# The first up weight of each next large expert is split before the present activation is transposed

## The chip, the cores and the metric

The kernel runs on one core of a Trainium2 chip. The metric is the device time of one execution in microseconds (us); three runs of the kernel before gave 2371.76 to 2372.97 us, with a median of 2372.91 us.

## What is computed

The reference is a block of three parts on 512 tokens of width 1024, in fp32: a mixer (attention over selected keys beside a state space model), a mixture of 32 experts with four experts for each token, and a second block of two further mixers. The change touches the mixture of experts alone. Cut to what matters, `toks` being the tokens of one expert `e`:

```python
def run_block(args):
    toks, e = args
    xb = h_pad[toks]
    gu = xb @ w_gu[e] + b_gu[e]
    g, u = gu[:, :D_EXPERT], gu[:, D_EXPERT:]
    g = jnp.minimum(g, SWIGLU_LIMIT)
    u = jnp.clip(u, -SWIGLU_LIMIT, SWIGLU_LIMIT)
    act = (u + 1.0) * (g * jax.nn.sigmoid(SWIGLU_ALPHA * g))
    return act @ w_dn[e] + b_dn[e]
```

Each expert's output is multiplied by the tokens' gates and added to their rows. `w_gu[e]` is 1024 x 2048 (8 MB), `w_dn[e]` is 1024 x 1024 (4 MB).

## The kernel before

The experts are ranked by their number of tokens and worked one after the other, each in a *turn*. The 17 ranks 0 to 16 are *large* (up to 128 tokens), the other 15 *small* (up to 64). `TURNS` sets the order: rank 0, then small and large in turn, with two places where two large ones follow each other. So 16 of the turns after the first belong to large experts.

An expert's weights come as 1 MB pieces: eight of `w_gu` (128 rows by 2048 columns each) for the products *up*, four of `w_dn` for the products *down*. `wraw` (L1704) issues a piece's load on SP's queue (L1709) into a ring of 11 buffers, named raw and XU in the profile; a buffer is free again once the piece has been used. The number of the expert is loaded into a register of SP at the start of its turn (`weights(i)`, L1795).

A large expert's products are made of three matmuls with fp32r operands (`mm3`, L387 to L389): the stationary operand, the activation, is held as a high part and a low part `hl`, and the moving operand, the weight, is split in the same way into H and L. `split` (L355) does that for a piece in two halves of 1024 columns: ScalarE casts the half to H (L368), VectorE subtracts H from the raw data to L (L370). H and L have three buffers each; every fourth half goes to a fourth pair, H2 and L2. The four groups of columns of a piece of `w_gu` go to four banks, two from each half; for each bank the order is H, L, H. A small expert's weights are used as they are, with no split (`up64` L1590, `down64` L1619).

A turn `i` (L1843 to L1878) does in this order: the up products of this expert (`up` or `up64`); the split of up to two down pieces of the previous expert, `down.begin`; the first part of the gate function (`glu`); the transposes of the next expert's gathered tokens (`transposed`, L1493, or `turned64`); the down products of the *previous* expert (`down.products`), in the midst of which the gate function is finished (`then`, L1603 and L1604); the selection matrix for the next expert's bias (`selected`, VectorE, L1690 or L1697); the transposes of this expert's activation (`acted` for a large one: eight transposes L1635, evictions on ScalarE L393 and VectorE L394; `turned` for a small one: four transposes L1506, one copy on ScalarE L1507), which the down products of the *next* turn use. `settle` runs `down.end`: the previous expert's output is scaled on VectorE (L1657) and added to its rows by a scatter that POOL issues (L1664). A large turn calls it behind the split of its first up piece (`then` in `up`).

From the second turn on, `inorder` (L305) ties each instruction of TensorE, VectorE and ScalarE to the one before it on its engine, so that these three engines keep the order in which the program is written. SP's and POOL's instructions are not tied.

Of the kernel before, what the change touches and what calls it, by code (L numbers as in the profile page):

```python
# [19 lines left out]
D = 1024  # L20
S = 512
NT = 4
KD = 8
# [7 lines left out]
NBIG = 17  # L31
# [3 lines left out]
def turns():  # L35
    big, small = list(range(1, NBIG)), list(range(NBIG, NE))
    gaps = max(1, len(small) - 1)

    upto = lambda k: (2 * k * len(big) + gaps) // (2 * gaps)
    more = [upto(k + 1) - upto(k) for k in range(gaps)]  # L40
    out = [0]
    for k, r in enumerate(small):
        out.append(r)
        if k < gaps:
            out, big = out + big[:more[k]], big[more[k]:]
    return out


TURNS = turns()
# [217 lines left out]
class Kern:  # L267
# [1292 lines left out]
        nc.vector.tensor_tensor(self.gate[:, r:r + 1], ms[:, :, 1], ms[:, :, 2], op=OP.add)  # L1560
        return u

    def up(self, hl, sel, pieces, pool=(), then=None):


        nc = self.nc
        bs = [self.bank("mm") for _ in range(4)]
        for k, c0, w, n in pieces:
            w = self.split(w(), n, pool=k in pool)
            if then and k == pieces[0][0]:  # L1570
                then()
            x = (hl[:, 0, k * P:(k + 1) * P], hl[:, 1, k * P:(k + 1) * P])
            for i in range(c0 // 512, (c0 + n) // 512):
                self.mm3(bs[i], x, w(i * 512 - c0, 512), k == 0, False)
                if k == KD - 1:
                    nc.tensor.matmul(bs[i], lhsT=sel[:, i // 2], rhs=self.bgu[:, (i % 2) * 512:(i % 2 + 1) * 512], start=False, stop=True)
            self.tick(1)
        return bs
# [168 lines left out]
    def moe(self):  # L1747
        nc, I, c, p = self.nc, self.I, self.c, self.p
        sel = self.sel0
        oh = self.oh0  # L1750
        with self.tc.issue_after(self.first.ins):
            hl = self.rows(oh)
# [26 lines left out]
        def following(i):  # L1779
            if i == 0:  # L1780
                self.route()
                yield
                self.slot(0, self.counted([oh], self.meta, 0, 1))
                yield from fetch(1)
                yield
            yield from fetch(i + 2)
            if TURNS[i] >= NBIG:
                yield from fetch(i + 3)

        def weights(i):  # L1790

            g, d = I["w_gu"][0], I["w_dn"][0]
            if i:
                r = TURNS[i]
                ev = nc.sync.value_load(self.eidi[:1, r:r + 1], min_val=0, max_val=NE - 1)  # L1795
                g, d = (I[n][bass.ds(ev, 1)].rearrange("o k n -> (o k) n") for n in ("w_gu", "w_dn"))
            return lambda k: g[k * P:(k + 1) * P], lambda kk: d[kk * 256:(kk + 1) * 256].rearrange("(p k) n -> p (k n)", k=2)

        def selected(i):
            r = TURNS[i]  # L1800
            return (self.select64 if r >= NBIG else self.select)(self.eid[:, r:r + 1])
# [38 lines left out]
        def settle():  # L1840
            while due:
                due.pop(0)()
        for i, r in enumerate(TURNS):  # L1843
            small = r >= NBIG
            wg, wd = weights(i)
            self.bg = [following(i)]
            with self.inorder(i > 0, (ET.PE, ET.DVE, ET.Activation), order):
                if small:
                    settle()
                    bs = self.up64(hl, sel, wg)  # L1850
                else:
                    with ExitStack() if i else self.tc.issue_after(self.first.ins):
                        bs = self.up(hl, sel, [(k, 0, lambda k=k: self.wraw(wg(k)), 2 * D) for k in range(KD)], then=settle)
                if i == 0:
                    self.rowload(self.gf, self.mrow[3], nc.gpsimd)
                    for h in range(2):
                        row = self.mrow[3]
                        nc.gpsimd.dma_start(self.gf2[64 * h:64 * h + 64], bass.AP(tensor=row.tensor, offset=row.offset + 512 * h, ap=[[0, 64], [1, 512]]))
                self.drain()
                if down:  # L1860
                    down.begin(0 if down.small else 2 if small else 1)
                glus = [self.glu(*bs)] if small else [self.glu(bs[n], bs[2 + n]) for n in range(2)]
                if i + 1 < NE:
                    hl = (self.turned64 if TURNS[i + 1] >= NBIG else self.transposed)(out.pop(i + 1))
                us = []
                then = lambda: us.extend(g() for g in glus)
                if down:
                    down.products(then)
                    due.append(down.end)
                else:  # L1870
                    then()
                osel = sel
                if i + 1 < NE:
                    sel = selected(i + 1)
                    if TURNS[i + 1] >= NBIG:
                        settle()
                ah = self.turned(us[0]) if small else self.acted(us)
                down = Down(r, ah, osel, wd)  # L1878
# [478 lines left out]
```

## Time and profile before

| | before |
|---|---|
| median of the runs | 2372.91 us |
| the profiled execution's own time | 2369.02 us |
| its span in the profile | 2366.8 us |
| VectorE busy | 1523.1 us (64% of the span) |
| ScalarE busy | 984.9 us (42%) |
| GpSimd busy | 309.1 us (13%) |
| bytes that the DMA engines moved | 576.36 MB |
| loads of expert weights | 256 of `w_gu`, 128 of `w_dn`, 1 MB each |

The profile names the engines PE (TensorE), PEld (its weight loads), DVE (VectorE), ACT (ScalarE), POOL (GpSimd) and SP (SyncE, which issues the loads). All times in it are counted from the start of the span. The expert stage lies between about 650 and 1705 us. A tile name such as H or raw stands for all of its buffers. The granted clock is a share: 1.00 is full speed, 0.50 half.

### The profile page before, as it was taken

What the parts mean: (1) busy time and instruction counts of PE and PEld (TensorE: products, weight loads), DVE (VectorE), ACT (ScalarE), POOL (GpSimd) and SP (SyncE); (2) the same over time, 40 slices, a digit from 0 to 9 for tenths busy, and PEclk for the clock granted to TensorE, in tenths of its full rate; (3) what the DMA queues carried; (4) which work ended last, traced back from release to release, by engine and by line L of the source; (5) the groups of instructions that cost most, each with busy time, mean ns of one, the idle gap of its engine ahead of it and who ended that gap; (6) DMA issues with size and microseconds to landing.
All of it is one profiled execution on the core that took longest, in us unless ns stands there. A gap on an engine that the chain in (4) does not pass through costs nothing. (4 is left out here: it accounts for less than half of the span.)

```text
span 2366.8 us, 28018 instructions
## 1 busy us (share of the span) xinstructions
PE 2224.0 (94%) x10217; PEld 1592.0 (67%) x10217; DVE 1523.1 (64%) x2471; ACT 984.9 (42%) x1371; POOL 309.1 (13%) x177
## 2 busy tenths in 40 slices
PE   5999999999799999999999999999879999999898
PEld 4676667677665566656566666665458888888676
DVE  7678778863866668766667667666451534448864
ACT  4424444332444436444444445444242422336652
POOL 3011102421111100101100010011010111101210
PEclk9999999999899999999999999999979999999999
DMA  7332344652899999999999998999732222222220
GB/s 303 99 106 103 122 158 164 242 176 87 328 390 372 400 402 393 353 387 388 392 405 396 398 403 336 378 407 393 292 145 74 103 83 82 88 83 96 91 87 36
DMA packets 93938, 576.36 MB, mean 244 GB/s; under 512 B 12591, under 2 KB 14361, under 8 KB 32611
## 3 DMA queue, kind: packets, MB, share of 16 engines
q1 hardware_dynamic: 79856, 540.60, 58.4%
q0 software_dynamic: 8432, 18.21, 3.1%
q10 hardware_dynamic: 5508, 15.71, 1.8%
q8 instruction: 82, 1.34, 0.2%
q14 instruction: 60, 0.49, 0.1%
HBM read 556.74 MB, written 27.59 MB: 247 GB/s over the span
## 5 line engine op out<-in xcount | busy, mean ns | idle before, releaser
L370 DVE TENSOR_TENSOR L<-raw,H 128x1024 fp32r<-128x1024 f32 x478 | 590.1, 1259 | 286.1 <-ACT H L368 277.3
L368 ACT CAST H<-raw 128x1024 fp32r<-128x1024 f32 x501 | 515.6, 1049 | 396.2 <-PE mm L389 179.4
L387 PE MATMUL mm<-H,hl 128*128 128x512 f32 x544 | 223.4, 411 | 25.9 <-ACT H L368 25.9
L388 PE MATMUL mm<-L,hl 128*128 128x512 f32 x544 | 225.0, 414 | 14.3 <-DVE L L370 14.3
L389 PE MATMUL mm<-H,hl 128*128 128x512 f32 x544 | 222.2, 408 | 0.0
L387 PE MATMUL mm<-U,H 128*128 128x512 f32 (+1 forms) x488 | 187.6, 384 | 3.0 <-DVE U L708 3.0
L388 PE MATMUL mm<-U,H 128*128 128x512 f32 (+1 forms) x488 | 186.6, 382 | 0.0
L389 PE MATMUL mm<-U,L 128*128 128x512 f32 (+1 forms) x488 | 185.7, 382 | 0.0
L1590 PE MATMUL mm<-raw,sx 128*64 128x512 f32 x792 | 180.3, 598 | 0.0
L387 PE MATMUL mm<-E,H 128*128 128x512 f32 x416 | 173.6, 420 | 3.7 <-ACT E L393 3.7
L387 PE MATMUL mm<-H,U 128*128 128x512 f32 x424 | 170.0, 401 | 2.3 <-DVE w L2256 1.1
L389 PE MATMUL mm<-H,U 128*128 128x512 f32 x424 | 168.2, 397 | 0.4 <-DVE U L394 0.4
L388 PE MATMUL mm<-E,H 128*128 128x512 f32 x416 | 167.0, 402 | 1.5 <-DVE E L394 1.4
L388 PE MATMUL mm<-L,U 128*128 128x512 f32 x424 | 168.3, 397 | 0.0
L389 PE MATMUL mm<-E,L 128*128 128x512 f32 x416 | 166.3, 400 | 0.0
L387 PEld LDWEIGHTS mm<-H,hl 128*128 128x128 f32 x544 | 107.0, 197 | 53.0 <-ACT H L368 29.0
L388 PEld LDWEIGHTS mm<-L,hl 128*128 128x128 f32 x544 | 107.5, 198 | 45.6 <-DVE L L370 21.0
L1599 ACT ACTIVATE w<-w 128x512 f32<-128x512 f32 x49 | 31.0, 632 | 248.4 <-DVE w L1598 248.4
L389 PEld LDWEIGHTS mm<-H,hl 128*128 128x128 f32 x544 | 107.7, 198 | 23.7
L1590 PEld LDWEIGHTS mm<-raw,sx 128*64 128x64 f32 x792 | 54.1, 137 | 98.6 <-issue 94.5
L370 POOL TENSOR_TENSOR L<-raw,H 128x1024 fp32r<-128x1024 f32 x23 | 55.2, 2401 | 444.5 <-ACT H L368 444.5
L388 PE MATMUL at<-L,hl 128*128 128x512 f32 x272 | 108.2, 398 | 2.3 <-DVE L L370 2.3
(443 smaller groups left out, 3843.0 us busy)
## 6 DMA issues: line engine op xcount, KB each, us to landing
raw<-in_w_gu_dram SPq DMA_DIRECT2D x212, 1024.0 KB
raw<-in_w_dn_dram SPq DMA_DIRECT2D x103, 1024.0 KB
XU<-in_w_gu_dram SPq DMA_DIRECT2D x44, 1024.0 KB
XU<-in_w_dn_dram SPq DMA_DIRECT2D x25, 1024.0 KB
raw<-in_win_dram SPq DMA_DIRECT2D x20, 1024.0 KB
raw<-in_w_ada_dram SPq DMA_DIRECT2D x16, 1024.0 KB
raw<-in_wug_dram SPq DMA_DIRECT2D x16, 1024.0 KB
raw<-in_wxg_dram SPq DMA_DIRECT2D x12, 1024.0 KB
```

The source lines that it names most:

```text
L368: nc.scalar.copy(h[:, :m], src)
L370: eng.tensor_tensor(l[:, :m], src, h[:, :m].bitcast(F32), op=OP.subtract)
L387: t.matmul(out, lhsT=lhs[0], rhs=rhs[0], start=start, stop=False)
L388: t.matmul(out, lhsT=lhs[0], rhs=rhs[1], start=False, stop=False)
L389: t.matmul(out, lhsT=lhs[1], rhs=rhs[0], start=False, stop=stop)
L1590: nc.tensor.matmul(bs[i // 2][64 * (i % 2):64 * (i % 2) + 64], lhsT=x[:, k], rhs=w[:, i * 512:(i + 1) * 512], start=False, stop=k == KD - 1)
L1599: nc.scalar.activation(s, g, AF.Sigmoid, scale=1.702)
```

## The change

Behind the down products of a turn, if there is a next turn, the kernel now makes the next expert's `weights`; if that expert is large, it also issues the load and the split of its first `w_gu` piece there, ahead of `selected`, of `settle` and of the transposes of the present activation. `up` gets the split piece as `head` and uses it in place of its own first split. The number of instructions stays the same.

```diff
-    def up(self, hl, sel, pieces, pool=(), then=None):
+    def up(self, hl, sel, pieces, pool=(), then=None, head=None):
...
         for k, c0, w, n in pieces:
-            w = self.split(w(), n, pool=k in pool)
+            w = head if head and k == pieces[0][0] else self.split(w(), n, pool=k in pool)
...
+        head, ahead = None, weights(0)
         for i, r in enumerate(TURNS):
             small = r >= NBIG
-            wg, wd = weights(i)
+            wg, wd = ahead
...
-                        bs = self.up(hl, sel, [(k, 0, lambda k=k: self.wraw(wg(k)), 2 * D) for k in range(KD)], then=settle)
+                        bs = self.up(hl, sel, [(k, 0, lambda k=k: self.wraw(wg(k)), 2 * D) for k in range(KD)], then=settle, head=head)
...
-                osel = sel
+                osel, head = sel, None
                 if i + 1 < NE:
+                    ahead = weights(i + 1)
+                    if TURNS[i + 1] < NBIG:
+                        head = self.split(self.wraw(ahead[0](0)))
                     sel = selected(i + 1)
                     if TURNS[i + 1] >= NBIG:
                         settle()
```

## Rows read from the trace of the kernel before

**Rows 1.** The page: TensorE's busy time, and its granted clock in 40 slices.

```profile
PE 2224.0 (94%) x10217; PEld 1592.0 (67%) x10217; DVE 1523.1 (64%) x2471; ACT 984.9 (42%) x1371; POOL 309.1 (13%) x177
PEclk9999999999899999999999999999979999999999
```

**Rows 2.** Waits of TensorE, 660 to 1700 us: who waited for whom, total, times, longest.

```profile
PE mm L387 <- ACT H L368: 25.9, 16, 1.6
PE mm L388 <- DVE L L370: 14.3, 20, 0.8
PE at L388 <- DVE L L370: 2.3, 2, 1.2
```

**Rows 3.** Time line of TensorE, 880 to 891 us: start, length, what, [idle before].

```profile
883.10 0.40 PE L389 MATMUL at<-H,hl 128*128 128x512 f32 x1
...
886.35 0.63 PE L1506 MATMUL at<-cst,w 128*128 128x128 f32 x4
888.60 0.50 PE L387 MATMUL mm<-H,hl 128*128 128x512 f32 x1 [1.62 <-ACT H L368]
889.86 0.50 PE L388 MATMUL mm<-L,hl 128*128 128x512 f32 x1 [0.76 <-DVE L L370]
```

**Rows 4.** Time line of ScalarE, 878 to 892 us.

```profile
881.10 1.05 ACT L368 CAST H<-raw 128x1024 fp32r<-128x1024 f32 x1 [0.41 <-PE at L389]
887.02 0.58 ACT L1507 COPY sx<-at 128x512 f32<-128x512 f32 x1 [4.87 <-PE at L1506]
887.50 3.89 ACT L368 CAST H<-raw 128x1024 fp32r<-128x1024 f32 x4
```

**Rows 5.** Time line of VectorE, 878 to 893 us.

```profile
882.43 2.35 DVE L370 TENSOR_TENSOR L<-raw,H 128x1024 fp32r<-128x1024 f32 x2
884.70 0.35 DVE L1690 TENSOR_SCALAR sel<-rc,eid 128x256 fp32r<-128x256 f32 x1
888.58 2.36 DVE L370 TENSOR_TENSOR L<-raw,H 128x1024 fp32r<-128x1024 f32 x2 [3.53 <-ACT H L368]
890.86 1.40 DVE L1657 SCALAR_TENSOR_TENSOR w<-at,gate,gf 128x512 f32<-128x512 f32 x2
892.18 1.21 DVE L370 TENSOR_TENSOR L<-raw,H 128x1024 fp32r<-128x1024 f32 x1
```

**Rows 6.** Time line of TensorE, 826 to 828 us, at another large turn's second weight.

```profile
826.07 0.40 PE L387 MATMUL mm<-H,hl 128*128 128x512 f32 x1
826.30 0.39 PE L388 MATMUL mm<-L,hl 128*128 128x512 f32 x1
...
827.69 0.51 PE L388 MATMUL mm<-L,hl 128*128 128x512 f32 x1 [0.53 <-DVE L L370]
```

**Rows 7.** 12 us from a gap: busy us (instructions) by engine, PEclk, DMA share, GB/s.

```profile
885.30:897.30 12.00, 9.62 (x36) 7.45 (x35) 8.72 (x9) 7.75 (x9) 2.32 (x1) 0.86 1.01 420
...
1060.90:1072.90 12.00, 9.62 (x31) 7.36 (x30) 8.29 (x8) 6.82 (x8) 2.33 (x1) 0.72 1.02 423
...
1194.80:1206.80 12.00, 9.08 (x40) 6.85 (x39) 8.65 (x9) 8.41 (x9) 2.33 (x1) 1.00 1.01 423
```

**Rows 8.** Time line of TensorE, 1064 to 1072 us, behind another gap.

```profile
1067.38 0.63 PE L389 MATMUL mm<-H,hl 128*128 128x512 f32 x1
1067.81 0.63 PE L387 MATMUL mm<-H,hl 128*128 128x512 f32 x1
```

**Rows 9.** The expert stage and two stretches of 20 us in it, columns as above.

```profile
660.00:1690.00 1030.00, 987.40 (x4446) 635.46 (x4447) 694.27 (x904) 470.81 (x530) 101.30 (x59) 0.98 0.98 388
...
760.00:780.00 20.00, 20.00 (x86) 16.20 (x86) 17.32 (x16) 12.62 (x12) 2.34 (x1) 0.97 1.02 400
...
1120.00:1140.00 20.00, 17.62 (x70) 13.84 (x69) 15.71 (x19) 12.51 (x15) 2.33 (x1) 0.91 1.01 420
```

**Rows 10.** Waits of SP's queue, 660 to 1690 us.

```profile
SPq L1709 <- DVE L L370: 420.5, 163, 6.2
```

**Rows 11.** Time line of SP, 860 to 876 us.

```profile
862.07 7.89 SPq L1709 DMA_DIRECT2D raw<-in_w_gu_dram  x5
```

**Rows 12.** Waits of ScalarE, 660 to 1700 us.

```profile
ACT H L368 <- DMA raw<-in_w_dn_dram: 27.0, 18, 3.6
```

## The prediction

> **What bounds the kernel now.** I read the page first, then the waits of TensorE, then the time line around one of them, then the transfers. TensorE is busy for 94% of the span, and its clock is granted in full over most of it [rows 1]. The chain that ended last goes back only to 1717.86 us, behind the expert stage, so it says nothing of the change and the stage has to be read by its waits. Between 660 and 1700 us TensorE's matmuls waited 25.9 us in 16 places for a cast of a weight on ScalarE, and 14.3 us in 20 places for a subtract on VectorE; there is little else [rows 2]. Sixteen is the number of turns that lead into a large expert. So TensorE sets the pace of the stage, and it loses it at the start of each large expert.
>
> One such place shows why. TensorE issues the last matmul of the third down weight at 883.10, works through the fourth, turns the activation at 886.35 with four transposes that last until 886.98, and then idles 1.62 us until the first weight's H half is there (888.60) and 0.76 us more for its L half [rows 3]. ScalarE was done with its last cast at 882.15 and stood idle for 4.87 us: the program order puts the copy of the turned activation first, and that copy needs the transposes. Only behind it come the casts of the first weight [rows 4]. VectorE idled 3.53 us for the same reason [rows 5].
>
> **The change, part by part.** Moved per large turn: one 1 MB load (its issue), two casts of 1.05 us and two subtracts (2.36 us together [rows 5]), from behind the transposes' evictions to ahead of them. Nothing is added or removed.
>
> *ScalarE.* Halves of a weight go in turn through three H buffers and one H2, so each is free again two weights later: the head needs what the third down weight held, whose last matmul ends at about 883.5 [rows 3]. ScalarE, idle from 882.15, can cast the head by about 884.9 (883.5, a wake-up of 0.4 as in the gap of [rows 4], 1.05), still 1.4 us before the transposes are issued. The copy behind it on ScalarE stays where it is.
>
> *VectorE.* It ends the fourth down weight's subtracts at 884.78; the head's two follow until 887.14, then the selection (0.35), the previous expert's output (1.40), and the first subtract of the second weight (1.21) until 890.10 [rows 5]. Late by this is only the selection, which the eighth weight's products need, far off; the previous expert's output, and POOL's scatter behind it, come 3.4 us earlier.
>
> *TensorE* finds H and the first L half (about 886.0) ready when the transposes end at 886.98. Both waits go: 16 x 1.62 = **25.9 us**, and the 0.77 us waits. Of the 14.3 us, four waits of 0.53 stand elsewhere (next paragraph), so 14.3 - 2.1 = **12.2 us**.
>
> *What is late next*: the second weight. Its second matmul would be issued at 886.98 + 13 x 0.23 = 890.0, and its L half is ready at 890.10, so some 0.2 us of wait. Today four of the sixteen places, those without the loss of clock below, wait 0.53 us there [rows 6]. I set this term to nothing; its ends are 16 x 0.2 = 3 us lost and 16 x 0.53 = 8.5 us won.
>
> *The clock.* After 12 of the 16 gaps the granted clock fell to half (1.2 instead of 2.4 GHz), and after none of the four others. In the 12 us from each gap, ten places have a mean clock of 0.86, two have 0.72 and four have 1.00. The places at 1.00 issued 39 or 40 matmuls, those at 0.86 about 3 fewer, those at 0.72 about 8 fewer [rows 7]. At 0.23 us each [rows 6] that is 10 x 3 x 0.23 + 2 x 8 x 0.23 = **10.6 us**. TensorE idles before each of these falls, so I take them to go with the gaps. Ends: nothing, if they come anyway; or 10 x 3.4 + 2 x 6.7 = 47 us at half clock (0.14 and 0.28 of 12 us, doubled), in which a matmul takes 0.43 instead of 0.23 us [rows 6, 8]: 47 x 0.46 = 22 us.
>
> *SP and POOL.* The register load of the next expert's number and the first weight's load are moved past no instruction of SP: between their old and new place stand only work of VectorE, ScalarE and TensorE, and the scatter on POOL. I cost this at nothing. The cover is the lead of the loads: the weight cast at 887.50 was issued at 862.07, 25 us before [rows 4, 11]. Without it the cast would wait for data, as the down weights' casts do now, 27.0 us in 18 places [rows 12].
>
> *The transfers.* They move 388 GB/s over the stage at a share of 0.98 [rows 9]. A stage 48.7 us shorter needs 388 x 1030 / 981 = 407 GB/s. Stretches of 20 us with a share above 1 show 400 to 420 [rows 9]. That is close, but SP's waits are for buffers (VectorE 420.5 us) [rows 10] and TensorE never waits for data there [rows 2], and the lead of 25 us can be eaten before it does. I take nothing; the other end is the second rival. The Trainium skill (HBM Reference, Specifications (TRN2)) gives an effective 358 GB/s per core, and about 425 for a core that streams alone; the 388 to 420 here agree with the second. By the first the loads would be at their limit already and the change would give nothing, by the second they stay clear.
>
> **Sum**: 25.9 + 12.2 + 10.6 = 48.7 us off the profiled 2369.0, which is 3.9 us below the median of the runs. Carried to the median: 2372.9 - 48.7 = **2324**.
>
> **Rivals.** (1) *As above*, 2324; own range from all of 25.9 + 14.3 + 22 = 62 us (2311) to a clock that falls anyway, 38.1 us (2335). Chance 0.66.
> (2) *The transfers become the bound.* If 400 GB/s [rows 9] is what they can do with the gathers and scatters among them, the stage loses only 1030 x (1 - 388/400) = 31 us: 2342. For it: the share near 1. Against: the lead, and the higher rows. 0.14.
> (3) *VectorE becomes the bound at the second weight.* If its chain is later than I work out, by the 0.77 of today, the wait for L moves one weight on and TensorE still idles enough for the clock to fall: only 25.9 us go, 2347. For it: just 0.1 us separate the two sums. Against: VectorE starts its subtracts 3.8 us earlier. 0.12.
> (4) *No change.* The transfers already set the pace, and what TensorE doesn't wait for here it waits for data later: 2373. Against it: no wait for data in [rows 2]. 0.04. By the 358 GB/s of HBM Reference (the Trainium skill, Specifications (TRN2)) it would come out so; the 388 GB/s of the stage [rows 9] speak against it.
> (5) *Slower: the head waits for its data.* The cast now stands ahead of the activation's eviction on ScalarE. Should the ring of loads run dry, so that the first weight lands over 2.4 us after the transposes end, each turn costs more than it saves. At the longest wait for data now, 3.6 us [rows 12], that is 16 x (3.6 - 2.4) = 19 us more: 2392. It takes the loss of a 25 us lead. 0.04.
>
> **How the numbers follow.** About 0.2% (4.7 us) is what a measurement of this kernel can tell from no change. Faster: (1), (2) and (3), 0.92; same: (4), 0.04; slower: (5), 0.04. The range runs from 2311, the far end of (1), to 2345, which takes in (2) and most of the way to (3); what lies outside is (4), (5) and part of (3).
>
> **What would show it.** Right: the 16 waits of L387 for the cast gone from TensorE's waits, the L388 waits for the subtract at 16 times 0.2 or less, the casts of the first weight ahead of the copy of the turned activation on ScalarE, no half clock between 690 and 1600 us, some 407 GB/s over the stage. Wrong: waits of a cast for w_gu data (2 or 5), L388 waits of 0.5 us and more at the second weight (3), or half clock without a gap before it.

## The result, and the profile after

| | before | after |
|---|---|---|
| median of the runs | 2371.35 us (6 runs) | 2343.82 us (6 runs, 2341.84 to 2347.54) |
| ratio to before, 95% interval | | 0.9888 [0.9875, 0.9902] |
| the profiled execution's own time | 2369.02 us | 2344.60 us |
| its span in the profile | 2366.8 us | 2342.4 us |
| the stage, share and rate of the transfers | 0.98, 388 GB/s [rows 9] | 1.00, 399 GB/s |

The change gains 27.5 us, where I forecast 48.7. The direction and the range were right, the size was not: 2343.8 is the time of rival (2), in which the transfers become the bound (2342). The page of the changed kernel shows little of this; TensorE's busy time, which answers to [rows 1], fell by 4.9 us, and the row of its clock looks much the same: slices of 59 us are too coarse for what happened.

```profile
PE 2219.1 (95%) x10217; PEld 1586.3 (68%) x10217; DVE 1519.0 (65%) x2471; ACT 983.1 (42%) x1371; POOL 295.3 (13%) x177
PEclk9999999999799999999999999999889999999999
...
q1 hardware_dynamic: 79856, 540.60, 58.7%
q0 software_dynamic: 8432, 18.21, 3.1%
```

The last two lines are the queue of the large loads and that of the gathers and scatters: packets, MB, share of the span on 16 engines. 18.21 MB take 3.1% (73 us of the span), 540.60 MB take 58.7%.

The waits of TensorE, 650 to 1700 us (who waited for whom, total us, times, longest), answer to [rows 2]:

```profile
PE at L388 <- DVE L L370: 13.9, 19, 1.2
PE at L387 <- ACT H L368: 8.9, 8, 1.5
PE mm L388 <- DVE L L370: 1.8, 2, 0.9
```

The 16 waits of an up product for its cast are gone, and so are the 0.76 us waits for the L half behind them. (The two waits left of an up product, 0.91 us each, stand at the second weight of the two large turns that directly follow a large one.) In their place stand 27 waits of the *down* products (`at`), 22.8 us, where [rows 2] have two of 2.3 us. The time line of TensorE around the place of [rows 3], one turn that lies 7 us earlier now, shows both:

```profile
872.86 0.40 PE L389 MATMUL at<-H,hl 128*128 128x512 f32 x1
873.88 0.50 PE L387 MATMUL at<-H,hl 128*128 128x512 f32 x1 [0.62 <-ACT H L368]
875.14 0.50 PE L388 MATMUL at<-L,hl 128*128 128x512 f32 x1 [0.76 <-DVE L L370]
...
881.38 0.63 PE L1506 MATMUL at<-cst,w 128*128 128x128 f32 x4
881.77 0.47 PE L387 MATMUL mm<-H,hl 128*128 128x512 f32 x1
882.08 0.39 PE L388 MATMUL mm<-L,hl 128*128 128x512 f32 x1
```

From the transposes to the first up matmul it is 0.39 us now (881.38 to 881.77), as forecast with no gap, and to the second 0.31. But the third down weight (873.88) comes late. ScalarE's time line says why:

```profile
863.77 1.99 ACT L368 CAST H<-raw 128x1024 fp32r<-128x1024 f32 x2 [13.10 <-DMA raw<-in_w_dn_dram]
867.21 2.00 ACT L368 CAST H<-raw 128x1024 fp32r<-128x1024 f32 x2 [1.45 <-DMA raw<-in_w_dn_dram]
871.29 0.63 ACT L1599 ACTIVATE w<-w 128x512 f32<-128x512 f32 x1 [2.08 <-DVE w L1598]
871.83 1.05 ACT L393 CAST hl<-at 128x512 fp32r<-128x512 f32 x2
872.77 4.88 ACT L368 CAST H<-raw 128x1024 fp32r<-128x1024 f32 x5
...
882.05 0.58 ACT L1507 COPY sx<-at 128x512 f32<-128x512 f32 x1 [3.01 <-PE at L1506]
```

The cast of the first down piece waited 13.10 us for the piece to land. ScalarE works in program order, so the gate function (871.29; it waited 2.08 us for VectorE, which stood behind the subtracts of these pieces), an eviction (871.83) and the casts of the later down pieces (872.77) run late behind it. The copy of the turned activation (882.05) does stand behind the head's casts, as the change asks. Over the stage, such waits of ScalarE have grown from 27.0 us, longest 3.6 [rows 12] (and 8.3 us, longest 2.7, for pieces in XU), to:

```profile
ACT H L368 <- DMA raw<-in_w_dn_dram: 139.5, 22, 15.4
...
ACT H L368 <- DMA XU<-in_w_dn_dram: 37.5, 6, 15.9
```

What SP waited for before it could issue a load, 650 to 1700 us, is the clearest sign. In [rows 10] its largest wait was for VectorE to free a buffer. Now the two largest are for earlier loads to land:

```profile
SPq L1709 <- DMA raw<-in_w_gu_dram: 209.6, 119, 4.3
SPq L1709 <- DMA raw<-in_w_dn_dram: 174.9, 80, 3.7
SPq L1709 <- PE mm L1590: 113.8, 73, 13.4
SPq L1709 <- DVE L L370: 95.7, 75, 5.0
```

With the buffers in XU, SP's waits for earlier loads come to 471.3 us, where the kernel before has 3.1; from 650 to 800 us there are none.

So two things happened: the gaps went, and the loads became the pace of the stage. The experiments separate the two.

### The profile page after: what moved, and what is told of

The parts are those of the page before. It is cut to its first block, busy times and chain, and to the rows that moved or that the text cites. A ratio compares the mean times of both kernels' runs of the same rounds, so it can differ in the third digit from the quotient of the medians.

```text
span 2342.4 us, 28018 instructions
## 1 busy us (share of the span) xinstructions
PE 2219.1 (95%) x10217; PEld 1586.3 (68%) x10217; DVE 1519.0 (65%) x2471; ACT 983.1 (42%) x1371; POOL 295.3 (13%) x177
## 2 busy tenths in 40 slices
DMA packets 93938, 576.36 MB, mean 246 GB/s; under 512 B 12591, under 2 KB 14361, under 8 KB 32611
## 3 DMA queue, kind: packets, MB, share of 16 engines
q1 hardware_dynamic: 79856, 540.60, 58.7%
q0 software_dynamic: 8432, 18.21, 3.1%
## 5 line engine op out<-in xcount | busy, mean ns | idle before, releaser
L388 PE MATMUL mm<-L,hl 128*128 128x512 f32 x544 | 215.3, 396 | 1.8 <-DVE L L370 1.8
L387 PE MATMUL mm<-H,hl 128*128 128x512 f32 x544 | 215.5, 396 | 0.0
L389 PE MATMUL mm<-H,hl 128*128 128x512 f32 x544 | 214.1, 394 | 0.0
L388 PE MATMUL mm<-U,H 128*128 128x512 f32 (+1 forms) x488 | 186.9, 383 | 0.0
L388 PE MATMUL mm<-E,H 128*128 128x512 f32 x416 | 167.6, 403 | 1.5 <-DVE E L394 1.4
L388 PE MATMUL mm<-L,U 128*128 128x512 f32 x424 | 168.7, 398 | 0.0
L388 PE MATMUL at<-L,hl 128*128 128x512 f32 x272 | 112.7, 415 | 14.1 <-DVE L L370 13.9
L388 PEld LDWEIGHTS mm<-L,hl 128*128 128x128 f32 x544 | 102.2, 188 | 29.2 <-DVE L L370 7.1
L387 PE MATMUL at<-H,hl 128*128 128x512 f32 x272 | 111.0, 408 | 8.9 <-ACT H L368 8.9
L387 PEld LDWEIGHTS mm<-H,hl 128*128 128x128 f32 x544 | 102.4, 188 | 22.2
L389 PEld LDWEIGHTS mm<-H,hl 128*128 128x128 f32 x544 | 102.1, 188 | 22.4
```

Of the source, the lines that this page charges most:

```text
L387: t.matmul(out, lhsT=lhs[0], rhs=rhs[0], start=start, stop=False)
L388: t.matmul(out, lhsT=lhs[0], rhs=rhs[1], start=False, stop=False)
L389: t.matmul(out, lhsT=lhs[1], rhs=rhs[0], start=False, stop=stop)
```

## The experiments

My theory (T) was that a gap is worth what I took or more, and that the transfers take back the rest. The rival (R) was that a gap is simply worth less, some 1.7 us instead of 3. All times are medians, and the ratio is taken over all runs, so it can differ a little from that of the two medians. Kernels with the same time in the column "before" were run beside the same runs of the kernel before. That column varies by 2 us, so a difference between kernels of different groups is good to some 2 us.

| kernel | us | before | ratio, 95% interval |
|---|---|---|---|
| few_after | 2302.12 | 2369.36 | 0.971 [0.9694, 0.9726] |
| few_before | 2366.75 | 2369.36 | 0.9988 [0.9978, 0.9999] |
| head_first8 | 2353.30 | 2369.36 | 0.993 [0.9913, 0.9946] |
| head_last8 | 2352.84 | 2369.36 | 0.9927 [0.9911, 0.9944] |
| noscatter | 2304.59 | 2370.14 | 0.9718 [0.9702, 0.9734] |
| spread | 2323.69 | 2370.14 | 0.9805 [0.9788, 0.9821] |
| early3 | 2354.56 | 2370.14 | 0.9934 [0.9917, 0.995] |
| ring4 | 2344.25 | 2370.14 | 0.9891 [0.9874, 0.9907] |
| spread_before | 2369.24 | 2371.38 | 0.9997 [0.9985, 1.0009] |
| spread_alt | 2323.36 | 2371.38 | 0.98 [0.9785, 0.9815] |
| spread_begin1 | 2325.61 | 2371.38 | 0.981 [0.9794, 0.9825] |

### Fewer loads, with the change and without it

On the changed kernel (few_after) and on the kernel before (few_before), 30 of the 384 loads of 1 MB fall away: the second and fourth down piece of each small expert, whose products read the first and third again. The instructions of TensorE, VectorE and ScalarE stay.

```diff
             def piece(d, kk):
-                w = self.wraw(d.wd(kk))
+                if d.small and kk % 2:
+                    return d.kept
+                w = d.kept = self.wraw(d.wd(kk))
                 return w if d.small else self.split(w)
```

> The changed kernel, with the second and the fourth down weight of each small expert left out (its products read the first and third again): 30 of 384 loads of 1 MB fewer, the same matmuls, casts and subtracts. T (the gaps were priced rightly, but the loads of weights became the bound once the lead of the loads was used up): the loads stop binding, so the full price of the gaps appears: 40 to 55 us under the kernel before (2371), with TensorE's waits for casts and subtracts nearly gone and the granted clock full through the stage. R (the gaps and the clock were worth only about half of what I took, and the loads play no part): the same 27 us as the change, within 5.

> The kernel before with the same 30 loads left out (second and fourth down weight of each small expert). T: the kernel before waits for the activation's eviction and not for data, so nothing moves: within 5 us of 2371. Rival D (the loads already held up the kernel before): 15 us or more faster.

Measured: 2302.12 and 2366.75. Without the change the missing loads are worth 0.12% and TensorE's waits stand as in [rows 2]; with it they are worth 41.7 us (2343.82 to 2302.12; 39.7 us with each set against the kernel before of its own group). So the kernel before was not held by its loads, and the changed one is. Between the two kernels with few loads lie 64.6 us: that is what the sixteen gaps cost, more than my 48.7 and more than twice what the change gave. R falls. The stage of few_after keeps no wait for a cast, and its clock never drops behind the start (waits of TensorE, 650 to 1660 us):

```profile
PE at L388 <- DVE L L370: 2.4, 2, 1.2
...
PE mm L388 <- DVE L L370: 1.8, 2, 0.9
```

How the gain goes is seen in three stretches of the stage (columns as in [rows 9]; the number to follow is the count of TensorE's matmuls, the first in brackets). Before:

```profile
640.00:860.00 220.00, 210.28 (x950) 134.62 (x952) 145.75 (x204) 96.87 (x110) 22.88 (x14) 0.98 1.00 391
860.00:1060.00 200.00, 191.68 (x862) 126.20 (x859) 140.72 (x187) 95.46 (x107) 19.05 (x12) 0.97 0.97 379
1060.00:1430.00 370.00, 354.64 (x1597) 226.82 (x1595) 246.02 (x321) 165.39 (x186) 36.19 (x21) 0.98 0.99 396
```

The changed kernel, and its stage as a whole:

```profile
640.00:860.00 220.00, 218.13 (x1010) 138.16 (x1010) 150.90 (x219) 100.01 (x113) 24.05 (x15) 0.99 1.01 401
860.00:1060.00 200.00, 193.96 (x882) 130.77 (x879) 151.61 (x194) 105.99 (x119) 17.94 (x12) 0.99 1.01 404
1060.00:1430.00 370.00, 357.56 (x1615) 227.90 (x1614) 250.57 (x330) 168.48 (x191) 29.94 (x22) 0.98 1.00 398
...
660.00:1665.00 1005.00, 981.49 (x4470) 626.76 (x4470) 693.00 (x907) 469.84 (x532) 90.18 (x60) 0.99 1.00 399
```

few_after:

```profile
640.00:860.00 220.00, 217.81 (x1008) 137.37 (x1006) 148.07 (x213) 101.85 (x116) 24.06 (x15) 0.99 1.00 389
860.00:1060.00 200.00, 197.92 (x910) 136.43 (x910) 159.28 (x200) 108.14 (x120) 20.45 (x12) 1.00 0.98 383
1060.00:1430.00 370.00, 367.92 (x1711) 236.61 (x1711) 263.42 (x349) 179.81 (x204) 38.70 (x23) 1.00 0.98 382
```

In the first 220 us the changed kernel does as much as few_after (1010 and 1008 matmuls, before 950). Then the lead of the loads is used up: 882 to 910 (before 862), and from 1060 to 1430 us 1615 to 1711, hardly more than the 1597 of before. (Some records of matmuls may be missing, and a cut falls in another part of a turn in each kernel, so a difference of some twenty means nothing.) The share of the transfers tells the cases badly apart: 0.98 stands in the stage before, which they did not bind, and in few_after.

### One half of the turns alone

```diff
-                    if TURNS[i + 1] < NBIG:
+                    if TURNS[i + 1] <= 8:
```

for head_first8, and `8 < TURNS[i + 1] < NBIG` for head_last8: each has eight of the 16 heads.

> The change at the first eight of the sixteen large turns alone (ranks 1 to 8). T: the stage gains some 4 us a turn until the lead of the loads is used up after five to six turns, and keeps that: 19 to 25 us under the kernel before. R (each gap is worth 27/16 = 1.7 us): 14 us, within 3.

> The change at the last eight of the sixteen large turns alone (ranks 9 to 16). T: the lead of the loads is still whole when they come, and the pair of large turns among them gives some of it back: 22 to 30 us under the kernel before, about as much as all sixteen. R: 14 us, within 3.

Measured: 16.1 and 16.5 us won, 8 waits of 1.62 us left in each. T's sizes are missed on both; by these two runs alone R would have stood, and it is few_after that rules it out. The halves sum to 32.6, over the 27.5 of both together, which is T's sign, but each gives half and not nearly all. The likely reason is that the limit is local: head_first8 has already fallen to 879 matmuls between 860 and 1060 us (the changed kernel 882), and what its loads have to spare in the second half can't be fetched ahead, because the ring holds 11 pieces. I have not shown that by a run of its own.

### Without the scatters

The output rows of the experts are not added to the tokens; the large loads stay as they are.

```diff
     def scatter(self, o, tok, small=False):
 
+        return
```

> The changed kernel with the 31 scatters that add an expert's output to its rows left out, so that the experts' outputs but the last are missing from the sum. T (the transfers bind): gathers and scatters hold the DMA engines for 3.1% of the span, about 73 us, for 18 MB; without the scatters some 30 us of that go to the weights' loads: 20 to 35 us under the changed kernel (2344), that is 2309 to 2324. Rival B (only the 1 MB loads count, the small packets fit between them): within 5 us of 2344.

Measured: 2304.59, 39 us under the changed kernel and within 2.5 us of few_after. That is more than I expected. TensorE's waits are those of few_after, SP waits for buffers again, and all transfers together run at 402 GB/s over the stage. The third line is the queue that in the changed kernel held the gathers and scatters, with 18.21 MB and 3.1%:

```profile
SPq L1710 <- DVE L L370: 369.5, 159, 5.7
```

```profile
660.00:1640.00 980.00, 975.63 (x4516) 627.68 (x4515) 697.83 (x912) 474.38 (x534) 41.95 (x29) 1.00 0.99 402
```

```profile
q0 software_dynamic: 3968, 9.90, 1.2%
```

So the full set of loads fits into a stage without gaps, if the scatters leave the transfers alone. The scatters are 8.31 of the 18.21 MB of queue q0, 1.4% of all bytes: at the 399 GB/s of the stage they would take 21 us by estimate. But they held the 16 engines for some 45 us (3.1% of 2342.4 us less 1.2% of 2303.1), and without them 39 us come back. Removing them also frees POOL (41.95 us busy, 90.18 with them), but nothing on TensorE waited for it.

### The rows of gathers and scatters spread over the partitions

A token's slot decides the partition in which its row lies. With fewer tokens than slots, the rows fill the first partitions. Here the slots are numbered in bit-reversed order, so that the rows spread over all partitions that a transfer covers (64 in a small expert's gather); rank 0 stays as it was.

```diff
-    parts["iota64"] = np.broadcast_to(i % 64, (P, P))
+    rev = lambda n: np.array([int(format(c, f"0{n}b")[::-1], 2) for c in range(1 << n)])
+    parts["slot64"] = np.broadcast_to(rev(6), (P, 64))
+    parts["slot128"] = np.broadcast_to(rev(7), (P, P))
...
-        return self.nc.vector.tensor_tensor(oh, self.mcc("iota64" if small else "iota128")[:, None, :].to_broadcast([P, NT, P]),
+        if small:
+            return self.nc.vector.tensor_tensor(oh.rearrange("p t (h c) -> p t h c", h=2), self.mcc("slot64")[:, None, None, :].to_broadcast([P, NT, 2, 64]),
+                                                pos[:, :, r:r + 1, None].to_broadcast([P, NT, 2, 64]), op=OP.is_equal)
+        return self.nc.vector.tensor_tensor(oh, self.mcc("slot128" if r else "iota128")[:, None, :].to_broadcast([P, NT, P]),
...
```

> The changed kernel with each expert's tokens put into its slots in bit-reversed order, so that the valid rows of a gather or scatter lie evenly over the partitions instead of in the first ones; the same bytes and instructions. T with uneven engines (the sixteen engines of a transfer serve fixed partitions, and those of the first partitions carry all gathers and scatters, so they finish the loads late): 10 to 30 us under the changed kernel (2344). T with even engines (only the sum of the work on all sixteen counts): within 4 us of 2344. R (transfers play no part): within 4 us.

The same edit on the kernel before is spread_before:

> The kernel before with the bit-reversed slots, without the moved split. T (the loads bind only once the gaps are gone): within 4 us of the kernel before (2370). Rival D (the slots make the kernel faster by themselves, whatever the gaps): some 20 us under it, as the slots gave the changed kernel.

Measured: with the change 2323.69, 20.1 us under the changed kernel; without it 2369.24 against 2371.38, a ratio of 0.9997 [0.9985, 1.0009], no difference. The order of the slots is worth something only where the transfers set the pace, so it acts through them. With spread_alt below, which is as fast, this is the fastest version of the study that computes everything, faster than both kernels. Its stage moves 406 GB/s, 7 more than the 399 of the changed kernel, and SP's waits for earlier loads are fewer, though not gone:

```profile
SPq L1714 <- DMA raw<-in_w_gu_dram: 160.7, 96, 3.2
```

```profile
660.00:1640.00 980.00, 963.59 (x4434) 617.35 (x4434) 685.29 (x898) 464.96 (x526) 93.16 (x60) 1.00 1.01 406
```

Two more runs asked what is left on top of spread. spread_alt has the 64-row gathers of small experts alternate between partitions 0 to 63 and 64 to 127:

```diff
-    def gather(self, gidx):
-
-        x = self.w4()
+    def gather(self, gidx, p0=0):
+
+        x = self.w4()[p0:]
...
-            out[i] = self.gather(self.gidx[:64 if r >= NBIG else P, r:r + 1])
+            p0 = 64 * (r % 2) if r >= NBIG else 0
+            out[i] = self.gather(self.gidx[:64 if r >= NBIG else P, r:r + 1], p0)
...
```

> The changed kernel with bit-reversed slots (2324), in which the gathers of every second small expert also land in partitions 64 to 127 instead of 0 to 63. T with uneven engines: a small gather of some 45 rows then lies on all engines in turn, 4 to 10 us under 2324. T with a gather's rows dealt to the engines by their number: within 3 us of 2324.

spread_begin1 splits only one down piece ahead of the gate function, so that ScalarE's queue stands behind one late load and not two:

```diff
-                    down.begin(0 if down.small else 2 if small else 1)
+                    down.begin(0 if down.small else 1)
```

> The changed kernel with bit-reversed slots (2324), which in a small turn begins one down weight of the previous expert ahead of the gate function instead of two. T (the transfers still set the pace, TensorE's waits in the down products are only where that shows): within 4 us of 2324. Rival Q (the second cast, waiting for its data at the head of ScalarE's queue, holds up the gate function and the evictions behind it, and that costs the 16 us that TensorE waits there): 8 to 16 us under 2324.

Measured: 2323.36 and 2325.61, no gain from either. Which half of the partitions a small gather uses makes no difference here, so of the two forms of T the one with uneven engines misses its 4 to 10 us. spread_begin1 leaves ScalarE's casts waiting for down pieces as long as before (154.6 us, in spread 158.0), because the first piece still stands at the head of its queue; TensorE's waits in the down products stay too (15.7 and 15.8 us). So beginning one piece fewer wins nothing, but whether the blocked queue has a cost of its own beside the late loads is not shown.

### The start of the stage and the depth of the ring

early3 issues the first expert's first three down loads ahead of the routing, to fill the ring earlier:

```diff
-        self.ahead = ahead + [self.wraw(I["w_gu"][0, k * P:(k + 1) * P, :]) for k in range(3, KD)]
+        ahead += [self.wraw(I["w_gu"][0, k * P:(k + 1) * P, :]) for k in range(3, KD)]
+        self.down0 = [self.wraw(I["w_dn"][0, kk * 256:(kk + 1) * 256, :].rearrange("(p k) n -> p (k n)", k=2)) for kk in range(3)]
+        self.ahead = ahead
...
-                w = self.wraw(d.wd(kk))
+                w = self.down0.pop(0) if d.r == 0 and self.down0 else self.wraw(d.wd(kk))
```

> The changed kernel with the first three down weights of the first expert loaded right behind its up weights, ahead of the wait for the routing, in a stretch (620 to 640 us) in which the transfers' share is 0.60, 8 us of idle time. T: the loads are three further ahead, which counts once: 5 to 8 us under the changed kernel (2344). R: within 3 us of it.

Measured: 2354.56, 10.7 us *slower* than the changed kernel: a plain miss. Down pieces of an expert are used a turn after its up pieces, so three of the eleven buffers were held by pieces not yet needed. SP's time line (start, length, what) shows it:

```profile
633.64 18.39 SPq L1709 DMA_DIRECT2D raw<-in_w_gu_dram  x8
673.03 0.34 SPq L1709 DMA_DIRECT2D raw<-in_w_dn_dram  x1
```

Between 652.0 and 673.0 us no load was issued. Once loads set the pace, an idle stretch of theirs is lost for good. From 620 to 700 us the share of the transfers is 0.76, in the changed kernel 0.89, so they idle for some 19 of these 80 us against 9. That difference of 10 us has the size of the loss; no run of its own shows that it is all of it.

ring4 has one buffer fewer, 10 instead of 11:

```diff
-NRAW = 5
+NRAW = 4
```

> The changed kernel with 10 instead of 11 buffers in the ring of loads. T (the rate of the transfers binds, the ring only holds the lead): one transfer less of lead, 2 to 5 us over the changed kernel (2344). Rival L (each transfer's latency binds, so that the loads in flight set the rate): 10/11 of the rate from the point where the loads bind, some 40 us over it or more.

Measured: 2344.25, the same as the changed kernel, so rival L falls, and the 2 to 5 us of T can't be told from nothing. It is the rate of the transfers that binds, not how many are under way. SP's largest wait is for buffers here, though the time is that of the changed kernel:

```profile
SPq L1709 <- DVE L L370: 240.8, 138, 5.7
```

Its waits for earlier loads still come to 237.9 us (before 3.1). So what tells is that such waits are there at all, and not which wait is the largest. A deeper ring, which would lengthen the lead, was not tried on the chip.

## Why the prediction was right in direction and wrong in size

- **TensorE's waits at the first weight** went as worked out, on all 16 turns; ScalarE's and VectorE's order is the one I laid out. Rival (3) came at two turns alone, the 0.91 us waits at the second weight where a large turn follows a large one.
- **The price of a gap** was too small. Three of its terms were short, and the reason is how I read the rows. First, the idle time that a row shows is less than what the wait costs, since a matmul's shown length overlaps the next one (0.40 us long, 0.23 us apart [rows 6]): from the transposes to the first up matmul it took 2.25 us before (886.35 to 888.60) [rows 3] and takes 0.39 now, so 1.86 and not 1.62; to the second 1.26 before and 0.31 now, so 0.95 and not 0.77. Second, I set the second weight's wait to nothing, and the four waits of 0.53 us [rows 6] went too: in few_after only the two waits of L388 on `mm` after a large turn are left. Third, the clock: I counted the matmuls missing in stretches with a fall against the stretches without one, but those are the four that held the second weight's wait, so a part of the loss cancelled out. A half-clock stretch holds some 8 matmuls, each 0.43 instead of 0.23 us apart [rows 6, 8], which is 1.6 us, not 0.7. Worked out again: 10 turns of 1.86 + 0.95 + 1.6, four of 1.86 + 0.95 + 0.53, two with twice the clock's loss, 44.1 + 13.4 + 12.0 = 69.5 us. Measured between the two kernels with few loads: 64.6. This sum was made with the result known; some 2 us of its excess are the two waits left, each 1.1 us from start to start.
- **The clock** falls with the gaps: behind the start of the stage few_before has as many stretches with a fall as the kernel before, few_after none, and the changed kernel five, each behind a new wait of the down products for a cast (1.01 to 1.50 us). Three more of these waits (0.62, 1.04 and 1.20 us) saw no fall, as four of the sixteen gaps before; why is open. The first block shows 12 us from such a place (columns as in [rows 7]), the second TensorE's time line there, where 0.43 us lie between starts at the lower of the two levels, 1.2 GHz:

```profile
1042.00:1054.00 12.00, 11.71 (x45) 9.34 (x46) 11.29 (x14) 7.94 (x9) 1.61 (x1) 0.86 1.02 423
```

```profile
1041.03 0.50 PE L387 MATMUL at<-H,hl 128*128 128x512 f32 x1 [1.12 <-ACT H L368]
...
1045.68 0.63 PE L389 MATMUL at<-H,hl 128*128 128x512 f32 x1
1046.11 0.63 PE L387 MATMUL at<-H,hl 128*128 128x512 f32 x1
```

- **The step that failed** is "The transfers": "I take nothing". The transfers took back 37 to 42 us of the gain (64.6 - 27.5; few_after against the changed kernel). I had worked out that 407 GB/s would be needed and set beside it stretches of 20 us at 400 to 420; but those are the best stretches, and the whole stage must hold the rate, with all its gathers and scatters. It held 399. Rival (2) took 400 for that and came within 2 us; its sum does not use the price of the gaps, which no longer matters once the loads are the bound. It deserved the largest chance and got 0.14. So the time fell into the range not by the mechanism of (1) but because its upper end was drawn at 2345 to take in (2). For a forecast of 2324 that is luck, and so is it that the two errors, 16 us too little for the gaps and nothing for the transfers, partly cancel.
- **The lead of 25 us** [rows 4, 11] did what I said, but only once: it carried the first 220 us of the stage, and was then gone. And waits of SP for buffers [rows 10] say that the loads are not the bound yet; they do not say by how much.
- **No change** (4) and **slower** (5) did not come: casts waited for an up piece twice in the stage, 1.3 and 1.0 us (before twice too, 1.1 us together). The long waits for data stand at the down pieces, as in [rows 12], now up to 15.9 us.
- **The rule** that I weighed: the Trainium skill (HBM Reference, Specifications (TRN2)) gives an effective 358 GB/s per core, the share when both cores of a pair stream, and about 425 for a core alone. By the first the change would have given nothing, by the second the loads would have stayed clear. Neither came: the stage kept 399 (406 with the slots spread), and 423 over the 12 us shown above, so the second is the better one. The scatters take a part of the rest (noscatter); what else does is not shown.

Still open: the 20 us between spread (2323.7) and the limit of the computing engines (2302 to 2305), and the sizes of the two halves.

## What to carry to other kernels

Before a wait of the pacing engine is removed, work out the rate that the next resource would have to hold over the *whole* stage, with all of its traffic, and compare it with a mean and not with the best stretches; a lead of a few pieces covers a shortfall once, not every turn. Two cheap kernels settle such a case: the changed one with fewer loads, and the one before with the same loads missing. Read what releases the queue that issues the loads: when waits for landed loads appear beside those for free buffers, it is time to work on the transfers, small ones first.

## What the runs showed of the hardware that was not expected

- Small indirect transfers cost the large ones more than their bytes: leaving out the scatters, 8.31 of 576.36 MB, gave back 39 us of a stage of about 1000, about twice what their bytes take at the rate of the stage and near the 45 us for which they held the DMA engines.
- The order of the slots alone gave 20.1 us (2343.82 to 2323.69) where transfers bind, and nothing (0.9997 [0.9985, 1.0009]) where they don't. That the rows then spread more evenly over the DMA engines would fit, but no view of the profile shows it, and moving the 64-row gathers to the other half of the partitions changed nothing.
- Prefetching more of the wrong pieces was slower (early3, 10.7 us), and a ring of 10 was as good as one of 11.
